# A two-layer diffusion-transformer kernel: attention and retention heads in pairs, and more of layer 0's expert activations computed before the dense stage

## The chip, the cores and the metric

One core of a Trainium2 chip. The metric is the device time of one execution in microseconds (us). The engines are named as in the profile: PE (TensorE, matrix products), PEld (its weight loads), DVE (VectorE), ACT (ScalarE), POOL (GpSimd), SP (the engine that issues most DMAs).

## The reference, cut to what matters

Two layers work on 256 tokens of `x` and, in layer 0 only, on 256 tokens of context, each of width 1024. Each layer is a mixer (layer 0: latent attention beside retention; layer 1: a gated delta rule), then a PEER block. Of the parts that change:

```
softmax_attend:  p = softmax(q k^T * scale);  o = p @ v          # 8 heads of 64 value columns
retention:       scores = (q k^T) * decay;    o = scores @ v     # 8 heads of 64
peer(h):  s1, s2 = q1 @ k1^T, q2 @ k2^T       # 8 heads x 2 halves, 128 keys each
          v1, i1 = top_k(s1, 16); v2, i2 = top_k(s2, 16)
          sc, j  = top_k(v1[:, None] + v2[None, :], 16)          # 16 experts of 16384 per head
          gate   = softmax(sc)
          act    = gelu(u_tab[e_idx] . h)
          out    = sum(gate * act * v_tab[e_idx])
```

## The kernel before, in words

**First mixer.** `attend(h)` is a generator for one attention head: query and key projections, scores `s`, softmax on DVE and ACT, transposes `pt` on PE copied to `pT` by ACT, and at last the product with the values (`oa`), 64 columns wide, which fills one half of the 128 output partitions; `put` splits the result into a high and a low part for the output projection. `retain(hp)` does two retention heads: scores `rs` (contraction over 64 partitions), decay on DVE (`sd`), product with the values (`or`, 64 columns), then a group norm. Each head's matmuls are issued by themselves. `weave` and `pipe` interleave the generators: three attention heads at a time, and one step of retention (two pairs at a time) behind each step.

**PEER, `route`.** It does not gather experts for most tokens. For 128 chunks of 128 experts it computes activations of all tokens (`act`: 24 matmuls a chunk, 384 columns each in layer 0, 256 in layer 1), multiplies them by a dense weight table `W` of gates in DRAM, and multiplies by the value table (`f`). `choose` projects the queries (`pq`, PE), takes scores (`sc`) and finds the 16 largest of each (`top`, DVE: MAX8, FIND_INDEX8, MATCH_REPLACE8). `decode`, `place` and `slots` turn the picks into columns, and `spread` builds `W`: DVE and ACT make one-hot tiles `O` and `A`, PE multiplies them (`wp`), ACT copies the product to `wst`, a DMA on SP's queue writes it. In layer 0 this covers three token blocks; the fourth (`Rows`) gathers its 128 expert rows of u and of v by indirect DMAs on POOL's queue (`rowu`, `rowv`, 512 KB each) and reduces them on DVE, one slot per step of a generator `steps`.

**PEER, `Dense`.** A table of u or v is read by SP's queue, ACT makes its high part (`ush`, `vsh`), DVE its low part (`usl`, `vsl`), and each product is three matmuls (high x high, high x low, low x high). `early` computes the activations of the first chunks ahead of time (12 in layer 0, 24 in layer 1), all kept in SBUF: `LEAD` says how many of its steps (a quarter chunk, 6 matmuls, each) are issued between the choice and `decode`, the rest goes one step per step of `spread`. `run` then goes over all chunks: activations of a pair of chunks that are not done yet, `weighted` (load of v, product of gelu and W, splits), and the `f` matmuls of the pair before. `fill` puts other work at given chunks: layer 0's affine step on POOL at chunk 2, 56 units of modulation weights (`adat`, 512 KB each, one or two DVE reductions) every second chunk from 12 on, and the 136 gather steps evenly over chunks 8 to 119.

**What sets the order.** The code's order is a priority: the Tile framework plans the instructions, takes for each engine the first in the code that is ready by its own model and whose buffers are free, and fixes each engine's queue in that order. Work can so come earlier than the code has it: the last gather steps run at 1413 us, 325 us before the dense stage ends, though the code puts them at chunk 119 of 128. On the chip each queue is strictly in order.

Lines: the matmul call 256; splits 270 (ACT) and 273 (DVE or POOL); `attend` 641, `retain` 705; `route` 799, with `top16` 816 to 822, `project` 829, `choose` 868, `decode` 884, `place` 923, `spread` 954; `Dense.act` 1076, gelu 1088, `weighted` 1098 to 1108; the gathers 1042, their reductions 1049 and 1059; `fill` 1649 to 1668; affine 422 and 423.

Of the kernel before, what the change touches and what calls it, by code (L numbers as in the profile page):

```python
# [21 lines left out]
P = 128  # L22
D = 1024
# [12 lines left out]
EARLY = 12, 24  # L36
LEAD = 15, 45
BUFS = 2, 3
LO = 'v', 'v'
# [8 lines left out]
SB = 2  # L48
# [196 lines left out]
class Model:  # L245
# [219 lines left out]
    def mixer0(self, open_x, open_h):  # L465
# [173 lines left out]


        def attend(h):
# [42 lines left out]
            for s in range(2):  # L684
                pT = p.tile([P, 2 * (s + 1), T], F32, tag=f"pT{s}", name=f"pT{s}{h}")
# [19 lines left out]
        def retain(hp):  # L705
            p = pr_
            oo = None
            for z in range(2):
# [5 lines left out]
                rows = slice(z * 64, z * 64 + 64)  # L714
                sds = []
                for s, b0, dec in ((0, 0, ds), (1, 0, dc), (1, 2, ds)):
                    o = ps.tile([P, 2, T], F32, tag="ps", name=f"rs{h}{s}{b0}")
                    for sb in range(2):
                        k0 = (b0 + sb) * P
                        self.mm(o[:, sb, :], rk[rows, hp, k0:k0 + P], rq[rows, hp, s * T:(s + 1) * T])  # L720
                    sd = p.tile([P, 2, T], F32, tag="sd", name=f"sd{h}{s}{b0}", bufs=6)
                    nc.vector.tensor_mul(sd, o, dec)
                    sds.append((s, b0, sd))
                    yield
                if oo is None:
                    oo = ps.tile([P, T2], F32, tag="ps", name=f"or{hp}")
                for s, b0, sd in sds:
                    for sb in range(2):
                        first, last = sb == 0 and b0 == 0, sb == 1 and (s == 0 or b0 == 2)
                        self.mm(oo[rows, s * T:(s + 1) * T], rv[:, b0 + sb, h * 64:(h + 1) * 64], sd[:, sb, :], first, last)  # L730
                yield
# [24 lines left out]
        rest = pipe([retain(hp) for hp in range(4)], 2)  # L756
# [42 lines left out]
    def route(self, l, hs, parts, ps, first, pd, early, rows=None):  # L799
# [3 lines left out]
        wd = self.dram.tile([len(spread_tbs) * P // WG, P, NE, WG], F32, name=f"W{l}")  # L803
        es = ExitStack()
# [8 lines left out]
        kT = pq.tile([P, 16, P], F32, name=f"kT{l}", bufs=1)  # L813
# [13 lines left out]


        def project(part, j):
# [8 lines left out]
            q = pq.tile([P, N], F32, tag="q", name="pqs" + u)  # L838
# [5 lines left out]
            S = scores[part, j] = pq.tile([P, N], F32, tag="S", name="S" + u, bufs=SB)  # L844
# [23 lines left out]
        def choose(part):  # L868
            pr = pipe([project(part, j) for j in range(16)], 2)
# [14 lines left out]
        def decode(part):  # L884
# [13 lines left out]
            nc.vector.tensor_mul(g, g, gs.unsqueeze(2).broadcast_to([P, n * NH, TOPK]))  # L898

# [16 lines left out]
            nc.vector.tensor_tensor(rb, jf[:, 0], rb, ALU.subtract)  # L916
            If = p.tile([P, n, NH, 2, TOPK], F16, tag="If", bufs=min(2, len(parts)), name="If" + u)
# [5 lines left out]
        def place(tb, n):  # L923
# [8 lines left out]
            for w in (8, 4, 2):  # L932
                nc.vector.tensor_add(eq[:, :, :w], eq[:, :, :w], eq[:, :, w:2 * w])
            ii = p.tile([P, P], F32, tag="ii", name=f"ii{t}{n}")
# [51 lines left out]
        work = choose(0)  # L986
        for part, tbs in enumerate(parts):
            weave(work)
            if part + 1 < len(parts):
                work, lead = choose(part + 1), 2 * AHEAD  # L990
            else:
                eq_.close()
                work, lead = early(), LEAD[l]
            for _ in range(lead):
                next(work)
# [3 lines left out]
            for i, tb in enumerate(tbs):  # L999
# [4 lines left out]
                weave(spread(tb, SHARE[l]), until=work)  # L1004
# [58 lines left out]
    class Dense:  # L1063
        G = 2

        def __init__(self, m, l, hs, nb, pool, ring):
            self.m, self.l, self.hs, self.nb, self.p, self.ring = m, l, hs, nb, pool, ring
            self.g = {}


        def early(self, es, ps):
            self.pg = self.m.pool(es, f"gelu{self.l}", 1)
            return chain.from_iterable(self.act(c, ps, "ps") for c in range(self.ring))


        def act(self, c, ps, tag, early=True):
            m, nc, l = self.m, self.m.nc, self.l
            N = self.nb * P
            ur = self.p.tile([P, KD, P], F32, tag="ur", name=f"ur{l}{c}", bufs=2)
            nc.sync.dma_start(ur, m.a["p_u"][l, c])  # L1080
            us = m.split(self.p, ur, [P, KD, P], "us", bufs=BUFS[l], eng=nc.gpsimd if early and LO[l][c % len(LO[l])] == "p" else None)
            o = ps.tile([P, 512], F32, tag=tag, name=f"act{l}{c}")
            for k in range(KD):
                m.mm3(o[:, :N], (us[0][:, k, :], us[1][:, k, :]), (self.hs[0][:, k, :N], self.hs[1][:, k, :N]), k == 0, k == KD - 1)
# [642 lines left out]
```

## Time and profile before

| | us |
|---|---|
| median of 3 runs | 3143.77 (3142.84 to 3145.04) |
| the profiled execution | 3142.63 |
| its span, first to last instruction | 3140.7 |
| PE busy in the span | 2816.7 (90%) |
| DVE busy | 2305.4 (73%) |
| ACT busy | 1281.7 (41%) |
| POOL busy | 708.5 (23%) |
| mean granted TensorE clock | 0.940 of full speed |

A busy time is the time in which at least one instruction of that engine is under way. Matmuls overlap: a 512-column matmul is recorded as 0.39 us, but the next one starts 0.23 us later. So the number of matmuls in a stretch says more about PE's pace than its busy share. Stages by time: first mixer's heads about 190 to 331 us, output projection and norms to 390, layer 0's choice and spread to 706, its dense stage to 1740, the second mixer to 2246, layer 1's choice and spread to 2467, its dense stage to the end.

### The profile page before, as it was taken

How to read it: one execution, taken by the hardware profiler on the slowest of the kernel's cores; microseconds unless marked ns; L12 is line 12 of the kernel's file. 1: busy time of each engine (PE TensorE's matmuls, PEld its weight loads, DVE VectorE, ACT ScalarE, POOL GpSimd, SP SyncE). 2: the span in 40 equal slices, each digit the busy share in tenths (PEclk: the TensorE clock that was granted, in tenths of full speed). 3: DMA queues.
4: the chain of work that ended last, by engine and by line, in shares of the span. 5: the costliest groups of instructions: out<-in, count | busy, mean ns of one | idle time of the engine just before them, and what ended most of it. 6: DMA issues, size and time to landing. Idle time of an engine off the chain costs nothing.

```text
span 3140.7 us, 44585 instructions
## 1 busy us (share of the span) xinstructions
PE 2816.7 (90%) x16843; PEld 2443.3 (78%) x16843; DVE 2305.4 (73%) x4520; ACT 1281.7 (41%) x2145; POOL 708.5 (23%) x453
## 2 busy tenths in 40 slices
PE   8989895857999999999999887669887899999997
PEld 4756685746999998888999666668787689999997
DVE  2955689977999999994444587976799655555555
ACT  3234432753333333333333334322348454444443
POOL 2410130024545555540000234423310100000000
PEclk9999997978999999999999888779899899999999
DMA  6530321568999999994443122312336866667663
GB/s 229 187 108 21 114 75 61 198 245 307 378 382 380 384 397 400 400 362 156 156 156 118 57 63 78 95 48 81 115 128 237 264 216 210 213 210 213 210 213 108
DMA packets 257192, 626.02 MB, mean 199 GB/s; under 512 B 34800, under 2 KB 124016, under 8 KB 252496
## 3 DMA queue, kind: packets, MB, share of 16 engines
q1 hardware_dynamic: 217632, 478.58, 45.3%
q0 software_dynamic: 38768, 142.49, 11.7%
q8 instruction: 132, 2.16, 0.3%
q10 hardware_dynamic: 576, 2.10, 0.2%
q14 instruction: 84, 0.69, 0.1%
HBM read 574.86 MB, written 48.23 MB: 198 GB/s over the span
## 4 chain that ended last, share of the span: by engine, by line
PE 55%; DVE 27%; DMA 9%; issue 5%; ACT 3%; POOL 1%; SPq 0%; POOLq 0%; ACTq 0%; DVEq 0%
PE f L256 20%; PE act L256 20%; DMA ur<-p_u 3%; DMA vr<-p_v 3%; DVE adaj L343 2%; DVE usl L273 2%; DVE cv L1264 2%; PE dz L256 1%; DVE O L966 1%; DVE rowy L1059 1%; PE y L256 1%; DVE vsl L273 1%; DVE rowu L1049 1%; DVE gelu L1108 1%; PE s L256 1%
## 5 line engine op out<-in xcount | busy, mean ns | idle before, releaser
L256 PE MATMUL f<-vsh,gsh 128*128 128x512 f32 x1260 | 491.1, 395 | 36.0 <-ACT vsh L270 36.0
L256 PE MATMUL f<-vsl,gsh 128*128 128x512 f32 x1260 | 497.7, 395 | 12.7 <-DVE vsl L273 12.5
L256 PE MATMUL f<-vsh,gsl 128*128 128x512 f32 x1260 | 494.9, 393 | 0.0
L273 DVE TENSOR_TENSOR vsl<-vr,vsh 128x1024 fp32r<-128x1024 f32 x252 | 301.4, 1228 | 246.8 <-ACT vsh L270 246.3
L273 DVE TENSOR_TENSOR usl<-ur,ush 128x1024 fp32r<-128x1024 f32 x256 | 313.5, 1226 | 173.9 <-ACT ush L270 173.9
L270 ACT ACTIVATE vsh<-vr 128x1024 fp32r<-128x1024 f32 x252 | 256.6, 1053 | 339.1 <-PE f L256 233.9
L270 ACT ACTIVATE ush<-ur 128x1024 fp32r<-128x1024 f32 x256 | 270.4, 1056 | 280.3 <-PE act L256 210.4
L256 PE MATMUL act<-hp0h,usl 128*128 128x384 f32 x1024 | 346.0, 338 | 14.5 <-DVE usl L273 14.5
L256 PE MATMUL act<-hp0h,ush 128*128 128x384 f32 x1024 | 347.0, 339 | 0.6 <-ACT ush L270 0.6
L256 PE MATMUL act<-hp0l,ush 128*128 128x384 f32 x1024 | 345.4, 337 | 0.0
L256 PEld LDWEIGHTS f<-vsh,gsh 128*128 128x128 f32 x1260 | 239.0, 190 | 88.8 <-ACT vsh L270 42.1
L256 PE MATMUL act<-hp1h,usl 128*128 128x256 f32 x1024 | 293.6, 287 | 7.7 <-DVE usl L273 7.7
L256 PE MATMUL act<-hp1h,ush 128*128 128x256 f32 x1024 | 293.6, 287 | 5.5 <-ACT ush L270 5.5
L256 PE MATMUL act<-hp1l,ush 128*128 128x256 f32 x1024 | 292.2, 285 | 0.0
L256 PEld LDWEIGHTS f<-vsl,gsh 128*128 128x128 f32 x1260 | 239.3, 190 | 65.4 <-DVE vsl L273 19.2
L256 PEld LDWEIGHTS f<-vsh,gsl 128*128 128x128 f32 x1260 | 239.1, 190 | 49.6
L270 ACT ACTIVATE gsh<-gelu 128x384 fp32r<-128x384 f32 (+1 forms) x256 | 120.3, 471 | 376.4 <-DVE gelu L1108 342.3
L1042 POOL DMA_INDIRECT rowu<-p_ur,rowe x128 | 181.6, 1419 | 189.7 <-DVE rowa L1049 135.3
L1042 POOL DMA_INDIRECT rowv<-p_v,rowe x128 | 180.2, 1408 | 146.0 <-DVE rowy L1059 121.4
L256 PEld LDWEIGHTS act<-hp0h,usl 128*128 128x128 f32 x1024 | 193.8, 189 | 15.7 <-DVE usl L273 15.3
L256 PEld LDWEIGHTS act<-hp1h,usl 128*128 128x128 f32 x1024 | 199.1, 195 | 8.9 <-DVE usl L273 8.7
L256 PEld LDWEIGHTS act<-hp1h,ush 128*128 128x128 f32 x1024 | 198.9, 194 | 8.4 <-ACT ush L270 6.3
(770 smaller groups left out, 5970.8 us busy)
## 6 DMA issues: line engine op xcount, KB each, us to landing
ur<-p_u SPq DMA_DIRECT2D x256, 512.0 KB, 4.4
vr<-p_v SPq DMA_DIRECT2D x256, 512.0 KB, 4.4
adat<-ada_t SPq DMA_DIRECT2D x80, 512.0 KB, 7.1
W<-wst SPq DMA_DIRECT2D x20, 2048.0 KB, 7.1
w<-W SPq DMA_DIRECT2D x32, 768.0 KB, 9.5
wq<-p_wq SPq DMA_DIRECT2D x32, 512.0 KB, 3.4
dw<-dn_in SPq DMA_DIRECT2D x32, 512.0 KB, 3.4
w<-W SPq DMA_DIRECT2D x32, 512.0 KB, 5.6
```

Of the source, the lines that this page charges most:

```text
L256: self.nc.tensor.matmul(out, l, r, start=start, stop=stop)
L270: nc.scalar.activation(hi, x, AF.Copy)
L273: (eng or nc.vector).tensor_sub(lo, x, hi.bitcast(F32))
L343: nc.vector.tensor_tensor_reduce(j, w, self.crow[:, s, :], op0=ALU.mult, op1=ALU.add, scale=1.0, scalar=self.c["ada_c"][:, l, m, k:k + 1], ...
L966: nc.vector.tensor_tensor(pairs(O[:, n]), bc(n), iob.unsqueeze(1).broadcast_to([P, OH, 64, 2]), ALU.is_equal)
L1042: nc.gpsimd.indirect_dma_start(t, None, tabs[z], bass.IndirectOffsetOnAxis(ap=self.e[:, s:s + 1], axis=0))
L1049: nc.vector.tensor_tensor_reduce(u, u, self.h, op0=ALU.mult, op1=ALU.add, scale=1.0, scalar=0.0, accum_out=self.act[:, s:s + 1])
L1059: nc.vector.scalar_tensor_tensor(self.y, rows.pop((1, v)), self.g[:, v:v + 1], self.y, ALU.mult, ALU.add)
L1108: nc.vector.tensor_mul(gv, gv, w4[:, :, c % WC, :])
L1264: (nc.gpsimd if CONV[j] == "p" else nc.vector).scalar_tensor_tensor(co, xp[:, :ns, q:q + T], cw[:, j, q:q + 1], co, ALU.mult, ALU.add)
```

## The change

Three things, in words, then the diff's core.

1. *Heads two by two.* `attend` of an even head keeps its transposed probabilities; the odd head issues the value products of both, alternating between the two halves of the output columns. `retain` issues the score products of its two heads alternately (two PSUM tiles, contraction in partitions 0 to 63 and 64 to 127) and so for the value products. One `put` of 128 partitions in place of two of 64. Retention pairs are started at every third step.
2. *36 chunks ahead in layer 0* (12 before; layer 1 stays at 24). The steps of all but `KEEP` = 4 of them (128 steps in layer 0, 80 in layer 1) are issued beside the choice (one or two behind each step of `top` once the projections have all been issued: 51 in layer 0, 3 in layer 1), beside `decode` and `place` (4 at each of ten places in layer 0, 8 at each of six in layer 1) and beside `spread` until they are used up; the four kept chunks come last. While the choice is issued, the tables' low parts go to POOL, after that to DVE. Gelu results of chunks 4 to 35 go to DRAM by a DMA on ACT's queue, and come back in `run` by one on SP's queue, 192 KB each, through a ring of 6. The next chunk's table is asked for while the present one is multiplied.
3. *Pace.* The work at chunks is placed by a cost of 18 for a chunk whose activations are done and 36 for another: 24 modulation units over chunks 3 to 35, the other 32 over the rest; gather steps from chunk 32 on; the affine step at chunk 59; `c_row` at chunk 0. Both v tables of a pair are asked for before either is used.

```diff
-EARLY = 12, 24
-LEAD = 15, 45
+EARLY = 36, 24
+KEEP = 4
...
-            r0 = (h % 2) * 64
-            rows = slice(r0, r0 + 64)
+            if h % 2 == 0:
+                first.append(pTs)
+                return
+            both = (first.pop(0), pTs)
             o = ps.tile([P, T2], F32, tag="ps", name=f"oa{h}")
             for s in range(2):
                 nk = 2 * (s + 1)
                 for kb in range(nk):
-                    self.mm(o[rows, s * T:(s + 1) * T], VM[:, kb, h * 64:(h + 1) * 64], pTs[s][:, kb, :], kb == 0, kb == nk - 1)
-            put(h // 2, rows, o[rows])
+                    for z in range(2):
+                        self.mm(o[z * 64:z * 64 + 64, s * T:(s + 1) * T], VM[:, kb, (h - 1 + z) * 64:(h + z) * 64], both[z][s][:, kb, :], kb == 0, kb == nk - 1)
+            put(h // 2, slice(0, P), o)
...
+            for s, b0, own in ((0, 0, 0), (1, 0, 1), (1, 2, 0)):
+                os = [ps.tile([P, 2, T], F32, tag="ps", name=f"rs{hp}{z}{s}{b0}") for z in range(2)]
+                for sb in range(2):
+                    k0 = (b0 + sb) * P
+                    for z in range(2):
+                        self.mm(os[z][:, sb, :], rk[rows[z], hp, k0:k0 + P], rq[rows[z], hp, s * T:(s + 1) * T])
...
-        rest = pipe([retain(hp) for hp in range(4)], 2)
+        rest = pipe([retain(hp) for hp in range(4)], 2, 3)
...
+        pd, work = dense.p, dense.early(e2, ps)
+        beside = islice(work, (EARLY[l] - KEEP) * KD // 2)
...
+                if ends[0]:
+                    n += 1
+                    step(1 + n % 2)
...
-            for _ in range(lead):
-                next(work)
+        for part in range(len(parts)):
+            weave(choose(part))
+        eq_.close()
+        dense.by = None
...
-                weave(spread(tb, SHARE[l]), until=work)
+                weave(spread(tb, SHARE[l]), until=beside)
         weave(work)
...
+                if c < KEEP:
+                    self.gelu(c, o)
+                else:
+                    g = self.pg.tile([P, self.nb * P], F32, tag="gelus", name=f"gelus{l}{c}", bufs=3)
+                    nc.scalar.activation(g, o[:, :self.nb * P], AF.Gelu)
+                    nc.scalar.dma_start(self.away[c], g)
...
+            def fetch(c):
+                late = c >= NE - 2
+                vr = (self.p if late else pool).tile([P, D], F32, tag="ur" if late else "vr", name=f"vr{l}{c}", bufs=2)
+                nc.sync.dma_start(vr, m.a["p_v"][l, c])
+                if KEEP <= c < done:
+                    self.gelu(c, None)
+                return vr
...
+        cost = np.cumsum([18 if c < EARLY[0] else 36 for c in range(NE - 6)])
...
-            fill.setdefault(12 + 2 * i, []).append(lambda u=u: m.ada_unit(pa, *u))
+            n = 3 * KD
+            share = ahead_share * (0.1 + 0.9 * i / n) if i < n else ahead_share + (0.97 - ahead_share) * (i - n) / (len(units) - n)
+            fill.setdefault(at(share), []).append(lambda u=u: m.ada_unit(pa, *u))
...
-        fill[2] = [affine]
-        fill[5] = [lambda: m.silu_rows(pa)]
+        fill.setdefault(at(0.4), []).append(affine)
+        fill[0] = [lambda: m.silu_rows(pa)]
...
-            fill.setdefault(8 + i * 112 // (P + LAG), []).append(lambda: next(steps))
+            fill.setdefault(at(0.9 * ahead_share + (1 - 0.9 * ahead_share) * i / (P + LAG)), []).append(lambda: next(steps))
```

## Rows read from the trace of the kernel before

**Rows 1.** Stretches: us; busy us (count) of PE, PEld, DVE, ACT, POOL; clock; DMA share; GB/s

```profile
196.00:308.00 112.00, 112.00 (x486) 70.19 (x486) 62.69 (x123) 43.99 (x99) 0.00 (x0) 1.00 0.13 37
...
390.00:494.00 104.00, 103.22 (x506) 87.36 (x507) 89.91 (x630) 33.54 (x52) 35.76 (x17) 0.98 0.22 72
494.00:521.00 27.00, 12.07 (x49) 11.11 (x49) 26.90 (x181) 4.00 (x5) 0.00 (x0) 0.68 0.13 40
521.00:546.00 25.00, 10.99 (x59) 9.89 (x58) 24.69 (x49) 8.43 (x10) 0.00 (x0) 0.77 0.26 85
546.00:678.00 132.00, 101.05 (x1003) 89.15 (x1004) 131.74 (x146) 99.98 (x236) 0.13 (x1) 0.88 0.51 200
678.00:706.00 28.00, 7.73 (x45) 7.41 (x43) 11.83 (x6) 4.48 (x7) 18.66 (x10) 0.68 0.85 298
706.00:782.00 76.00, 59.77 (x227) 46.53 (x228) 57.75 (x82) 25.31 (x34) 33.30 (x25) 0.85 0.85 302
782.00:1740.00 958.00, 947.86 (x4799) 860.66 (x4798) 754.40 (x1037) 342.33 (x487) 332.07 (x234) 1.00 0.82 302
```

**Rows 2.** Groups of PE's instructions, 196 to 331 us: busy us, mean ns, idle before

```profile
L256 PE MATMUL rs<-rq,rk 64*128 64x256 f32 x96 | 27.6, 407 | 0.0
L256 PE MATMUL or<-sd,rv 128*64 128x256 f32 x96 | 22.4, 383 | 0.0
L256 PE MATMUL oa<-pT,VM 128*64 128x256 f32 x96 | 21.3, 382 | 0.0
```

**Rows 3.** Timeline of PE in the first mixer: start us, us, what

```profile
233.78 0.38 PE L256 MATMUL oa<-pT,VM 128*64 128x256 f32 x1
233.83 0.38 PE L256 MATMUL or<-sd,rv 128*64 128x256 f32 x1
233.99 0.38 PE L256 MATMUL oa<-pT,VM 128*64 128x256 f32 x1
```

**Rows 4.** Timeline of PE in the second mixer, 32-row tiles

```profile
2019.57 0.57 PE L256 MATMUL x<-r,Y 32*32 32x32 f32 x25
```

**Rows 5.** Chain of waits: pieces (start us, us, what), and shares by line for 678 to 800 us

```profile
615.01 1.26 PE wp L256 x22
...
by line: DMA vr<-p_v 33.4%; PE f L256 17.6%; PE act L256 9.4%; DMA W<-wst 8.6%; DVE gelu L1108 7.7%; DMA w<-W 7.4%; DVE vsl L273 3.9%; issue 3.6%; DVE gsl L273 3.5%; ACT vsh L270 3.5%; DVE rowu L1049 1.1%; ACT wst L981 0.4%; ACTq L270 0.1%;
...
678.07 10.48 DMA W<-wst
...
688.62 9.00 DMA w<-W
...
780.36 8.34 PE act L256 x48
788.71 8.20 PE f L256 x36
```

**Rows 6.** Groups of DVE's instructions, 782 to 1738 us

```profile
L1059 DVE SCALAR_TENSOR_TENSOR rowy<-rowv,rowg,rowy 128x1024 f32<-128x1024 f32 x124 | 158.6, 1279 | 3.4 <-DMA rowv<-p_v,rowe 3.4
...
L273 DVE TENSOR_TENSOR usl<-ur,ush 128x1024 fp32r<-128x1024 f32 x112 | 136.5, 1219 | 74.0 <-ACT ush L270 74.0
...
L343 DVE CUSTOM_DVE_ANT_0 adaj<-adat,c_row,small 128x1024 f16<-128x1024 f32 x74 | 94.5, 1278 | 1.1 <-DMA adat<-ada_t 1.1
...
L1108 DVE TENSOR_TENSOR gelu<-gelu,w 128x384 f32<-128x384 f32 x114 | 62.8, 551 | 0.9 <-ACT gelu L1088 0.8
```

**Rows 7.** Groups of POOL's instructions, 380 to 490 us (the choice)

```profile
L273 POOL TENSOR_TENSOR usl<-wq,ush 128x1024 fp32r<-128x1024 f32 x14 | 33.6, 2398 | 55.4 <-ACT ush L270 55.4
```

**Rows 8.** Groups of instructions, 540 to 700 us (spread and what follows)

```profile
L270 ACT ACTIVATE ush<-ur 128x1024 fp32r<-128x1024 f32 x10 | 10.6, 1056 | 12.4 <-DMA ur<-p_u 8.7 <-PE act L256 3.6
...
L1108 DVE TENSOR_TENSOR gelu<-gelu,w 128x384 f32<-128x384 f32 x2 | 4.4, 2255 | 3.1 <-DMA w<-W 3.1
```

**Rows 9.** A DMA issued by ACT: ns of the issue, min/median/max

```profile
L322 ACTq DMA_DIRECT2D xT<-xT x4: 335/430/454, 0.8 to 6.6; - x4
```

**Rows 10.** Layer 1's first dense stretch, columns as in rows 1

```profile
2467.00:2537.00 70.00, 67.89 (x291) 54.12 (x291) 42.27 (x62) 32.66 (x45) 0.00 (x0) 0.95 0.69 218
```

More of the change, by code (lines that the diff above doesn't have):

```diff
@@ L2 @@
 from contextlib import ExitStack
-from itertools import chain, count, cycle
+from itertools import chain, count, cycle, islice
 import numpy as np
@@ L47 @@
 SHARE = 5, 5
-SB = 2
 AHEAD = 1
@@ L638, in mixer0 @@
         p = self.pool(ea, "m0at", 3)
+        first = []
         def attend(h):
@@ L795, in query, with route @@
         return self.split(pool, w, [P, KD, P], "us", bufs=BUFS[l], eng=eng)
-    def route(self, l, hs, parts, ps, first, pd, early, rows=None):
+    def route(self, l, hs, parts, ps, first, dense, e2, rows=None):
         nc, a, c = self.nc, self.a, self.c
@@ L826, in route, with step @@
         rects = ((0, 1, 16, 0), (1, 3, 8, 16), (4, 4, 4, 40), (8, 8, 1, 56))
+        def step(n):
+            for _ in range(n):
+                next(beside, None)
         def project(part, j):
@@ L1091, in run, with ahead @@
-        def run(self, wd, done, pool, psa, psv, fill, sums=None, ready=None):
-            m, nc, l, nb, G = self.m, self.m.nc, self.l, self.nb, self.G
+            m, N = self.m, self.nb * P
+            self.pg = m.pool(es, f"gelu{self.l}", 1)
+            self.by = m.nc.gpsimd
+            self.away = {c: m.dram.tile([P, N], F32, name=f"gelud{self.l}{c}") for c in range(KEEP, self.done)}
+            return self.ahead([*range(KEEP, self.done), *range(KEEP)], ps)
+        def ahead(self, order, ps):
+            m, nc, l = self.m, self.m.nc, self.l
+            us = self.table(order[0])
+            for n, c in enumerate(order):
+                now, us = us, None
+                o = ps.tile([P, 512], F32, tag="ps", name=f"act{l}{c}")
+                for k in range(KD):
+                    self.product(o, now, k)
+                    if k == 1 and n + 1 < len(order):
+                        us = self.table(order[n + 1])
+                    if k % 2:
+                        yield
+                if c < KEEP:
[4 more added lines that the diff above has]
+                    nc.scalar.dma_start(self.away[c], g)
@@ L1093, in run, with act @@
+        def act(self, c, ps, tag):
+            us = self.table(c)
+            o = ps.tile([P, 512], F32, tag=tag, name=f"act{self.l}{c}")
+            for k in range(KD):
+                self.product(o, us, k)
+            self.gelu(c, o)
+        def run(self, wd, pool, psa, psv, fill, sums=None, ready=None):
+            m, nc, l, nb, G, done = self.m, self.m.nc, self.l, self.nb, self.G, self.done
             N = nb * P
@@ L1639, in build @@
         dense = m.Dense(m, 0, h, 3, *pools0, EARLY[0])
-        wd = m.route(0, h, ((0, 1, 2, 3),), ps, first, dense.p, lambda: dense.early(e2, ps), rows)
+        wd = m.route(0, h, ((0, 1, 2, 3),), ps, first, dense, e2, rows)
         ep.close()
@@ L1690, in build @@
             dense = m.Dense(m, 1, h, 2, *pools1, EARLY[1])
-            wd = m.route(1, h, ((0, 1),), ps, first, dense.p, lambda: dense.early(e2, ps))
+            wd = m.route(1, h, ((0, 1),), ps, first, dense, e2)
             ep.close()
@@ L1703, in affine @@
                     m.affine(nc.gpsimd, t, rows)
-            last = dense.run(wd, EARLY[1], *pools, {2: [affine]})
+            last = dense.run(wd, *pools, {2: [affine]})
             for tb in range(2):
```

109 lines of the change are left out of this document (52 added, 57 removed).

## The prediction

> **What bounds the kernel now.** I read the busy times by stretch first, to see which engine is full where. In the first mixer's heads PE is busy all 112 us, DVE 63, ACT 44. In the choice PE (103 of 104 us) and DVE are both full. From 494 to 678 us DVE is full in each of the three stretches and PE is not, at a granted clock of 0.68 to 0.88. From 678 to 706 everything waits, and from 706 to 782, the 12 chunks whose activations are ready, PE is busy 60 of 76 us. From 782 to 1740 PE is full at full clock [rows 1]. The chain of waits then says what a matmul costs back to back: 48 of `act` in 8.34 us and 36 of `f` in 8.20 us, each two chunks, so 4.17 and 4.10 us a chunk, 8.27 together; 958 us for 116 chunks is 8.26 [rows 1, 5]. That stretch is at PE's own pace, though DVE is busy 754 of 958 us and DMA at 302 GB/s.
>
> The sum is made against the profiled execution, 3142.63 us (span 3140.7 and 1.9 around it); the median is 3143.77, 1.1 more. About 0.2% (6.3 us) can be told from no change.
>
> **Part 1, heads in halves.** `rs`, `or` and `oa` are 96 matmul records each, and `oa` shows 21.3 us of them, 0.222 us a record [rows 2]. Three times 96 by 0.222 is 64 us of PE's 112. If two halves run side by side, up to 32 us go. For column halves a row exists: where `oa` and `or` happen to alternate, one starts 0.05 us behind the other and the pair takes 0.21 us, what one alone takes [rows 3]. For `rs`, whose halves are the contraction's, the nearest row is 32-row tiles: 25 small matmuls in 0.57 us, 0.023 us each, which a serial array would hardly do [rows 4]. So the gain lies between 0 and 32 us. I take 20: the value products in full (21), two thirds of `rs` (7), less 8 us, a quarter of the 32, for pairs that coincide already and for DVE (63 us) and ACT (44 us) taking turns in each head's chain once PE needs only 80. `put` of 128 partitions saves four copies and subtractions off the path; nothing counted. The Trainium skill's page TensorEngine Tiling (Array Packing), Key Properties, says that different tiles load and multiply in parallel; by it the sum would have all of `rs`, 4 us more. No row here shows 64-row tiles side by side.
>
> **Part 2, choice and spread.** 24 more chunks are 24 x 4.17 = 100 us of PE, moved from a stage where PE is full to one where it isn't. *PE:* until 494 it is full with projections, and the new steps are issued behind them. From 494 to 706 (212 us) it is busy 132 us, at a low clock [rows 1]. 768 `wp` at 0.057 us (22 in 1.26) are 44 us at full clock [rows 5], 12 chunks 50, the rest some 5: 99. With 100 more that is 199 at full clock, or 232 if the busy time of now stays: PE just has room, or is 20 us short. *DVE:* low parts of 36 tables; about 14 go to POOL (51 steps of a quarter chunk, and one table ahead), 22 stay against 12 now: 10 x 1.14 (start to start; 1.22 recorded [rows 6]) = 11 us in a stage that DVE fills, so the last spread product moves from 678 to about 690. *POOL:* 14 x 2.4 = 34 us beside the 36 it does in the choice [rows 1, 7]: room. It slows DVE there at most by its own 34 us, at least not at all. The row of contention is a product of two tiles that takes 2.26 us in place of 0.55 while POOL does the affine step [rows 6, 8]; the choice's MAX8 and FIND_INDEX8 have POOL's 36 us beside them now and DVE stays full, so I take 1. *ACT:* 24 high parts at 1.06 [rows 8] and gelus at 0.5, with 32 DMA issues at 0.43 [rows 9]: 50 us, with 95 free of 212 [rows 1]. *SP:* 24 more reads of u, where the DMA share is 0.13 to 0.51 [rows 1].
>
> *Then the join.* Now the last write of `W` takes 10.5 us and the read 9.0, then products slowed by POOL's affine step (DVE gelu 7.7% of 122 us, 9.4) [rows 5]. The affine step moves to chunk 59: 6 us less here, some 5 back there. The four kept chunks (16.7 us) fill the wait. First `f`: 706 + 11 + 1 - 6 + 6 for PE being tight = 718, +12. Bounds: -6, and +55 (20 for PE, 34 for POOL, 1).
>
> **Part 3, the dense stage.** 24 chunks lose 100 us of PE; 92 chunks at 8.26 remain, 760 us. The open price is a chunk whose activations are ready. PE needs 4.10 us; layer 1's such stretch gives 70 us for 24 chunks of 12 `f`, 2.92 against 2.73, a factor of 1.07 [rows 10], so 4.4 here; the 12 of now took 76 us, 6.33 each [rows 1], with a third of 122 us on the chain waiting for v's landing [rows 5]. A chunk now reads v (0.52 MB), its gelu (0.20), `W` (0.20, a quarter of 768 KB) and 24/36 of a modulation unit (0.35): 1.27 MB, at 4.4 us 288 GB/s, against 302 at a DMA share of 0.85 in the stretch of 6.33 [rows 1]. DVE needs low part and two short products, 2.3 us, and 48 reductions of 1.28 [rows 6] over 36 chunks, 1.7: 4.0, no slack. I take 5.0, nearer to layer 1's since the gathers have their place behind: 180 us. The gathers (two DVE operations of 1.2 to 1.3 us a slot [rows 6]) then have 760 us; now they end at 1413, within some 700 us and in the same company, with PE full, and DVE's whole load is 812 - 27 = 785 us of 945. They cost nothing under that cover; if DVE fell behind, they would be late before the last norm, up to 25 us. Affine step: 5. Stage: 180 + 760 + 5 = 945 against 1034: -89. Bounds -116 (4.4 us) and -21 (6.33, and 25 late).
>
> **Part 4, layer 1.** The same 24 chunks; 20 results go out and back (0.43 us of ACT each, 9 us beside PE and DVE), POOL takes one or two low parts, and the last four chunks fill the join as some do now. 0, bounds -6 and +8.
>
> **Sum:** -20 + 12 - 89 + 0 = -97: 3142.6 - 97 = **3046 us**. All good ends together give 2983, all bad ones 3185.
>
> **Rivals.**
> *A, the ready chunks stay held by DMA.* The pace is a priority only; before, the last gather ran 30 chunks early. If gathers, reloads and modulation crowd v again, 36 chunks cost 6.33: +48, 3094. For: the third of the chain on v's landing. Against: the first of these chunks also had 1 MB of affine rows, and the gather rings to fill. 20%.
> *B, the mixer's heads become bound by evacuation.* Pairs finish sooner, but every product must still be read by DVE or ACT, and each head's chain passes five times between engines: 5 us gained in place of 20, 3061. Against: DVE's 63 of 112 us. The Trainium skill speaks for it (TensorEngine Tiling (Array Packing), PSUM Bottleneck: tiling quickens the matmuls, not the copying out). 14%.
> *C, slower: activations stand in front of the spread.* PE's queue is in order and 75 of the 128 steps are issued before the first spread. When a table's low part waits in DVE's queue behind a spread group (132 us / 24 = 5.5 us [rows 1]), PE stands, the two buffers of `O` and `A` fill, and DVE stands as well. If each of the 22 tables on DVE costs a whole group: +121, 3167. It decides from 97/22 = 4.4 us a table. For: DVE is full there, and PE is not. Against: one table is asked for ahead, and the plan orders DVE's queue by the same priorities. 8%.
> *D, the halves do not run side by side* in this code: 3066. 7%, since rows 3 show it for columns.
>
> **How the numbers follow.** Forecast 47%, A 20, B 14, D 7, C 8; 4% for A with the bad ends of part 2, about no change. All but C and that are faster: 0.88; same 0.04; slower 0.08. The range from 3000 to 3105 holds the forecast but for its best corner, A, B and D; left out are C, the no-change case and part of the ends of A, together near 2 in 10.
>
> **What would show it.** Right: `rs`, `or`, `oa` near half their busy time, and the heads' stretch some 20 us shorter; PE at full clock from 494 on, with first `f` near 718 of the old clock (698 with the mixer's gain); 36 chunks in some 180 us; then 8.26 us a chunk to the end; gathers ending within 100 us of it. Wrong: a chain full of v's landing after the join (A), PE waiting on low parts among the spread (C), DVE or ACT releasing most of the heads' matmuls (B), or a tail in which the last norm waits for `rowy`.

## The result, and the profile after

The changed kernel takes 3102.4 us, the median of 4 runs (3091.6 to 3114.1), beside 3144.4 for the kernel before: ratio 0.9867, 95% interval 0.9823 to 0.9911; five more runs gave 0.9862 (0.9840 to 0.9884). So it is 42 us faster, where 97 were forecast. The profiled execution is the fastest of the four, 3091.57 us (span 3089.8), 50.9 less than the span before. Its marks, the first and last start or end of a tile in the timeline:

| | before | after | difference | forecast |
|---|---|---|---|---|
| first `pq` (end of the mixer) | 390.2 | 368.4 | -21.8 | -20 |
| first `pq` to first `f` | 316.0 | 352.3 | +36.3 | +12 |
| first `f` to last `f` (dense stage) | 1044.9 | 986.6 | -58.3 | -89 |
| last `f` to layer 1's first `pq` | 494.5 | 497.4 | +2.9 | 0 |
| layer 1's first `pq` to the end | 895.1 | 885.1 | -10.0 | 0 |

Stretches of the changed kernel (us; busy us and count of PE, PEld, DVE, ACT, POOL; clock; DMA share; GB/s), to be read against [rows 1]:

```profile
196.00:286.00 90.00, 84.74 (x466) 55.20 (x467) 62.69 (x130) 44.84 (x99) 0.00 (x0) 0.91 0.16 50
...
368.00:497.00 129.00, 126.16 (x632) 109.27 (x632) 114.08 (x807) 41.79 (x62) 48.06 (x23) 0.98 0.27 90
497.00:557.00 60.00, 54.80 (x299) 53.78 (x300) 51.09 (x60) 22.64 (x31) 24.52 (x9) 0.94 0.49 159
557.00:694.00 137.00, 121.73 (x1157) 111.43 (x1156) 136.15 (x144) 109.12 (x250) 0.00 (x0) 0.97 0.66 251
694.00:721.00 27.00, 18.38 (x106) 18.06 (x104) 7.64 (x9) 12.07 (x15) 8.94 (x9) 0.88 0.96 358
721.00:900.00 179.00, 171.19 (x739) 137.85 (x739) 166.36 (x265) 61.12 (x86) 23.47 (x16) 0.98 0.95 332
900.00:1020.00 120.00, 117.43 (x596) 106.82 (x595) 114.64 (x149) 42.03 (x62) 73.69 (x52) 1.00 1.01 387
1020.00:1080.00 60.00, 40.80 (x178) 35.71 (x179) 47.85 (x52) 11.72 (x18) 44.34 (x28) 0.84 0.76 284
1080.00:1480.00 400.00, 380.90 (x1880) 339.88 (x1880) 369.16 (x504) 133.40 (x200) 236.86 (x164) 0.99 1.02 385
1480.00:1700.00 220.00, 219.29 (x1122) 199.30 (x1121) 100.23 (x132) 79.84 (x110) 0.00 (x0) 1.00 0.43 135
```

What to see: the choice still ends some 130 us after the first `pq` (at 521 us before, 497 now), but decode and slots, which follow it, now take 60 us where they took 25 [rows 1]; PE, busy 11 of those 25 us, is busy 55 of the 60. From 1020 to 1080 PE runs 178 matmuls in place of some 300. From 1080 to 1480 it is busy 0.95, with DVE at 0.92 and the DMA share over 1. Only from 1480, with the last row reduced, is it at its own pace again: 1122 matmuls in 220 us are, at 42 a chunk, 8.24 us a chunk, beside a DVE less than half busy.

The mixer's groups, which answer to [rows 2]:

```profile
L254 PE MATMUL rs<-rq,rk 64*128 64x256 f32 x96 | 16.4, 447 | 0.0
L254 PE MATMUL oa<-pT,VM 128*64 128x256 f32 x96 | 13.5, 438 | 0.0
L254 PE MATMUL or<-sd,rv 128*64 128x256 f32 x96 | 11.2, 384 | 0.0
```

71.3 us of busy time became 41.1. The timeline of PE shows the pairs (start us, us, what):

```profile
240.36 2.81 PE L254 MATMUL oa<-pT,VM 128*64 128x256 f32 x24
247.12 2.81 PE L254 MATMUL or<-sd,rv 128*64 128x256 f32 x24
```

That is 0.117 us a record where one cost 0.222 [rows 2]: the two column halves run side by side. The two halves of the contraction do so as well for the most part (`rs` from 27.6 to 16.4). The Trainium skill, TensorEngine Tiling (Array Packing), Key Properties, says that different tiles can load and multiply in parallel, and the trace agrees.

The dense stage, cut where the 37th chunk's first `f` starts (648 of 2304 records lie before it), `f` alone (PE, PEld, DVE; clock; DMA share; GB/s):

```profile
720.60:900.40 179.80, 156.17 (x648) 122.37 (x649) 0.00 (x0) 0.98 0.96 332
900.40:1707.40 807.00, 398.30 (x1656) 314.29 (x1656) 3.38 (x5) 0.98 0.83 306
```

The first stretch looks like the 180 us of the forecast, but it also holds 93 records of `act` for the four chunks behind, 16.2 us of PE. Without them the 36 ready chunks take 163.6 us, 4.5 each where 5.0 was forecast. The other 92 take 807.0, where the same 92, with the same `act`, took 764.0 before: 43 us more, and the forecast had 5 more there, for the affine step. The table's shortfall of 31 us in the stage is smaller than that, since the ready chunks came cheaper. Two questions follow: what costs 43 us in the 92 chunks, and what costs 24 more than forecast in the route.

### The profile page after: what moved, and what is told of

It is laid out like the page before. It is cut to its first block, busy times and chain, and to the rows that moved or that the text cites. A ratio compares the mean times of both kernels' runs of the same rounds, so it can differ in the third digit from the quotient of the medians.

```text
span 3089.8 us, 44817 instructions
## 1 busy us (share of the span) xinstructions
PE 2792.0 (90%) x16843; PEld 2424.3 (78%) x16843; DVE 2307.7 (75%) x4500; ACT 1272.9 (41%) x2141; POOL 747.8 (24%) x469
## 4 chain that ended last, share of the span: by engine, by line
PE 38%; DVE 16%; DMA 11%; issue 6%; POOL 4%; ACT 3%; POOLq 0%; SPq 0%; ACTq 0%; DVEq 0%
PE f L254 16%; PE act L254 15%; DMA vr<-p_v 3%; DMA rowv<-p_v,rowe 3%; DMA ur<-p_u 2%; DVE cv L1322 2%; PE dz L254 2%; POOL rowv L1061 1%; POOL rowu L1061 1%; DVE vsl L271 1%; DVE usl L271 1%; DVE rowy L1078 1%; DVE adaj L341 1%; DVE rowu L1068 1%; DMA adat<-ada_t 1%
## 5 line engine op out<-in xcount | busy, mean ns | idle before, releaser
L271 DVE TENSOR_TENSOR usl<-ur,ush 128x1024 fp32r<-128x1024 f32 x240 | 295.0, 1229 | 165.3 <-ACT ush L268 161.5
L1061 POOL DMA_INDIRECT rowu<-p_ur,rowe x128 | 175.2, 1369 | 279.0 <-DVE rowa L1068 182.7
L1061 POOL DMA_INDIRECT rowv<-p_v,rowe x128 | 186.9, 1460 | 95.5 <-DVE rowy L1078 72.0
```

What stands on the lines that cost most here:

```text
L271: (eng or nc.vector).tensor_sub(lo, x, hi.bitcast(F32))
L1061: nc.gpsimd.indirect_dma_start(t, None, tabs[z], bass.IndirectOffsetOnAxis(ap=self.e[:, s:s + 1], axis=0))
```

## The experiments

Each run is compared with runs of the kernel before on the same chip; the ratio is to those. "Rest" below is the time of the last 92 chunks in the trace, cut as above; it then holds the same matmuls in every run for which it is given, but for `gathers_8`, where 46 more `act` records (some 8 us) fall behind the cut.

### The mixer alone

The kernel before, with `attend`, `retain` and their weaving from the change and nothing else.

> The kernel before with the mixer's edit alone (heads two by two). My step said -20; the changed kernel's first pq stands 21.8 us earlier. If the edit is worth that by itself: first pq at 368 to 369 in place of 390.2, 3120 to 3123 us. Rival B (evacuation sets the pace): some 5 us, 3138. Rival D (halves one behind the other): 3142 to 3144. If the two parts of the change are independent, the rest of the change is then worth about -20 of the -42 measured.

3121.1 us, ratio 0.9914 (0.9901 to 0.9926): 27 us less. First `pq` at 365.7, 24.5 earlier; the route behind it takes 316.0 us and layer 1 896.7, as before. So the halves are worth 21 to 27 us. Rivals B and D fall, and of the 42 us only about 15 are left for the rest of the change.

### Without the gathered rows

The changed kernel, and the kernel before, each without the steps of `Rows`:

```diff
-        for i in range(P + LAG):
-            fill.setdefault(at(0.9 * ahead_share + (1 - 0.9 * ahead_share) * i / (P + LAG)), []).append(lambda: next(steps))
```

> The changed kernel without the 256 gathers and their DVE operations (the fourth block's expert rows are left out, its sum stays zero). My step said that the gathers cost nothing under PE's cover. If so, the rest of the dense stage stays at 800 to 810 us and the total at that of the changed kernel. Theory T5 (the gathers are the whole loss of the step): 92 chunks at 8.26 to 8.30, 760 to 764 us, the total 40 to 48 less. Rival (reloads, order of splits and the affine step lose it): 785 to 805.

> The kernel before without the gathers and their DVE operations (the fourth block's expert rows left out). My step read them as free under PE's full queue. If free: dense stage 1035 to 1045, total within 10 us of the kernel before. If they cost there what they cost after (63 us): 3083. Between, theory T7: 12 ready chunks at 5 in place of 6.9 (-22) and the other 116 at 8.27 in place of 8.30 (-4), 3115 to 3122; then the change itself makes the gathers dearer by some 35 to 40 us, since the products moved away leave fewer chunks to carry the same 128 slots.

After: 3038.1 us, ratio 0.9664 (0.9643 to 0.9685), 63 less than the changed kernel's 3101.5. Before: 3113.9, ratio 0.9902 (0.9887 to 0.9916), 31 less. The `f` of the changed kernel without rows, cut at the same chunk:

```profile
716.50:889.10 172.60, 154.28 (x648) 121.00 (x649) 0.00 (x0) 0.99 0.92 306
889.10:1652.70 763.60, 387.82 (x1656) 310.76 (x1656) 3.38 (x5) 0.99 0.50 159
```

and of the kernel before without rows:

```profile
702.40:973.20 270.80, 153.82 (x648) 122.75 (x649) 0.00 (x0) 0.97 0.78 260
973.20:1722.40 749.20, 385.64 (x1656) 309.75 (x1656) 3.36 (x5) 1.00 0.46 144
```

Without rows the rest is 763.6 us, so the rows cost 43 us there and 7 in the ready chunks. They were not free before either: 15 us of these 92 chunks, 10 of the first 36. The change made them 25 (traces) to 32 us (medians) dearer.

The rest of the loss is not the rows': without them the 92 chunks still take 14 us more than in the kernel before (763.6 against 749.2). These lie in one place. The changed kernel without rows, with the columns of the first fence:

```profile
900.00:1000.00 100.00, 89.87 (x438) 81.08 (x438) 69.17 (x101) 29.36 (x42) 20.54 (x8) 0.95 0.71 246
1000.00:1100.00 100.00, 100.00 (x510) 91.34 (x509) 43.34 (x51) 35.68 (x49) 0.00 (x0) 1.00 0.51 161
```

From 1000 us on PE keeps its own pace, as in the kernel before without rows (3049 and 3050 matmuls from 1000 to 1600). The 72 matmuls that are missing from 900 to 1000 are 14 us. There lies the affine step, which POOL does from 898 to 921 us in this run, and behind it DVE waits for modulation tables (`adat`, 31.4 us from 885 to 1000). No run without rows has the affine step elsewhere, so which of the two it is stays open. The reloads can cost little: the ready chunks take 172.6 us, 4.3 each without the `act` among them, and PE alone needs 4.10.

### The affine step

```diff
-        fill.setdefault(at(0.4), []).append(affine)
+        fill.setdefault(2, []).append(affine)
```

> The changed kernel with the affine step issued at chunk 2 in place of chunk 59. Theory 1a (POOL's queue is in order, so the affine step in the midst of the gathers holds rows back, then low parts on DVE behind them, then PE): the hole of 1020 to 1080 us, 178 products against 280 to 300, closes, the rest of the dense stage falls by 20 to 25 us, the ready chunks lose 5 to 10: 15 us less in all. Rival 1b (gathers packed too densely for DMA and DVE, the affine step only the place where it shows): the hole moves or spreads, total within 6 us of the changed kernel.

3089.4 us, ratio 0.9824 (0.9806 to 0.9842), against 0.9862 some 12 us less. Rest 781.3 (25.5 less), ready chunks 190.0 (10 more), and 282 matmuls from 1020 to 1080 us in place of 178: close to what theory 1a had. What stood in the hole, on POOL of the changed kernel (timeline; idle time before and what ended it in brackets):

```profile
1032.50 0.61 POOL L387 DMA_DIRECT2D lb<-ln_b  x1
1033.41 1.61 POOL L1061 DMA_INDIRECT rowu<-p_ur,rowe  x1 [0.30 <-issue]
1040.95 13.47 POOL L421 TENSOR_TENSOR x<-x,lb 128x1024 f32<-128x1024 f32 x4 [5.92 <-DMA lb<-ln_b]
1054.57 0.95 POOL L1061 DMA_INDIRECT rowv<-p_v,rowe  x1 [0.15 <-issue]
```

and on DVE:

```profile
1045.45 3.41 DVE L271 TENSOR_TENSOR vsl<-vr,vsh 128x1024 fp32r<-128x1024 f32 x1
...
1061.59 1.28 DVE L1078 SCALAR_TENSOR_TENSOR rowy<-rowv,rowg,rowy 128x1024 f32<-128x1024 f32 x1 [9.38 <-DMA rowv<-p_v,rowe]
```

POOL waits for `lb` and then adds for 13.47 us; the next gather, behind it in the same queue, goes out 21 us after the one before it. DVE stands 9.38 us on that row, with the next low parts behind it, and PE on those (10.58 us on `usl`). A low part on DVE takes 3.41 us beside POOL's additions, in place of 1.22. How much of the 25.5 us is this hold on the gathers is not measured: up to 14 of them can be what shows without any rows.

### Spacing the rows

With the affine step at chunk 2 the rest is still 17 us over the 764, and 32 over the 749 of the kernel before without rows, which has its affine step at chunk 2 as well. Two explanations were tried: rows too dense for DVE and DMA, and too few row buffers. The pacing runs tie the rows to their chunk (`dense.last` is the latest low part of a gelu product), by their indices, four at a time, 4 slots ahead (`hard_pace`) or 12 (`soft_pace`, with the affine step at chunk 2):

```diff
+            def free(s):
+                if s % 4 == 0 and s < P:
+                    q = slice(s, s + 4)
+                    nc.vector.scalar_tensor_tensor(self.e[:, q], dense.last[:, :4].bitcast(F32), 0.0, self.ef[:, q], ALU.mult, ALU.add)
```

or by their products, four at a time (`hold`) or one (`hold_1`), both with the affine step at chunk 2, and `hold` with two more edits (`hold_combo`). `hard_pace` leaves the affine step at chunk 59.

```diff
+                if s % 4 == 0 and s < P:
+                    nc.vector.tensor_scalar(self.act[:, s:s + 4], dense.last[:, :4].bitcast(F32), 0.0, 0.0, ALU.mult, ALU.add)
```

> The changed kernel with each four gathers' indices written on DVE behind the latest chunk's split of its gelu, so that a gather cannot start before its chunk (32 small DVE operations, some 0.1 us each). Theory 1b: gathers stretch from 604 us to some 700 or more, DMA share falls from 1.03 to 1.05 towards 0.9, and the rest of the dense stage falls from 9.06 to 8.3 to 8.6 us a chunk: 40 to 60 us less. Theory 1a: the hole at the affine step stays, 10 to 20 us less. Rival T2 (reload and byte count or DVE's load itself, whatever the spacing): no gain, or up to 10 us more.

> The affine step at chunk 2, and the gathers held to their chunks as in the first pacing run, but with each four indices freed 12 slots ahead of their product in place of 4, so that a row has some 40 us to land in place of some 15. Theory 1b' (the first pacing run lost because a row's landing of 6 to 10 us stood inside the ring's round, and dense packing is what costs): gathers end near 1620, rest of the dense stage 765 to 775 us against 781 of the run with the affine step alone, 5 to 15 us less in all. Rival (a gather costs DVE's and DMA's time wherever it lies; spreading them over more chunks gives nothing): rest of the dense stage 778 us or more, total the same or slower.

> Affine step at chunk 2, and the rows' products (not their gathers) held to their chunks: every four results are first set to zero on DVE behind the latest chunk's gelu split, so the products of these slots cannot run ahead on DVE, while a row is fetched as soon as its buffer is free. Theory 1b'' (what costs is 1.9 slots a chunk, 4.7 us of DVE beside 3.5 for the chunk itself and the modulation units, more than a chunk's 8.27; at 1.5 a chunk DVE keeps up): gathers end near 1640, PE's share in 1000 to 1480 goes from 0.95 to 0.99, rest of the dense stage 765 to 772 against 781, total 8 to 16 less than with the affine step alone. Rival (rows in DVE's order cost PE their waits at any spacing, as both pacing runs had it): rest 790 or more, total longer.

> As the run that held the rows' products, but slot by slot in place of four at once (128 one-column DVE operations, some 0.1 us each, 13 us of DVE in all). If the groups of four were what cost there (products in bursts of four, a ring of three rows of v behind them): rest of the dense stage 770 to 790, total 3075 to 3095. If rows cost PE their waits whenever they are held to a place in DVE's order: rest 825 or more, total 3130 or more.

> The same with the quarter chunks behind the first block's slots and 5 low parts on POOL. If the gains add: 8 to 16 less than the run with the three edits, 3066 to 3075; by the rival longer than 3082.

| | us | ratio (interval) | rest | last row reduced |
|---|---|---|---|---|
| affine step alone | 3089.4 | 0.9824 (0.9806 to 0.9842) | 781.3 | 1479 |
| `hard_pace` | 3169.9 | 1.0079 (1.0064 to 1.0094) | 883.1 | 1640 |
| `soft_pace` | 3137.6 | 0.9976 (0.9964 to 0.9988) | 831.3 | 1572 |
| `hold` | 3147.9 | 1.0009 (0.9996 to 1.0021) | 842.3 | 1642 |
| `hold_1` | 3124.0 | 0.9922 (0.9905 to 0.9939) | 819.6 | 1631 |
| `hold_combo` | 3141.7 | 0.9985 (0.9974 to 0.9996) | 845.0 | 1634 |

All five lost, and my theory that a wider spacing would win is refuted in each form that was tried; each of them also ties the rows to a place in DVE's order, and none spaces them without that. Bursts of four are a part of it (`hold` to `hold_1`: 23 us of the rest), not the whole. One stretch, with the columns of the first fence, of the kernel with the affine step alone:

```profile
1200.00:1479.00 279.00, 263.56 (x1312) 235.22 (x1311) 257.18 (x353) 94.40 (x140) 161.96 (x111) 0.99 1.00 377
```

and of `hold_1`:

```profile
1200.00:1479.00 279.00, 263.65 (x1289) 235.10 (x1288) 222.03 (x333) 88.84 (x134) 142.39 (x96) 0.98 0.90 319
```

Paced, DVE has 57 us to spare and DMA a tenth, and still PE does fewer matmuls: the waits moved to `rowy` on the landing of v's rows (83.0 us in 900 to 1600, the list of waits). A fourth buffer for these rows, without pacing:

```diff
-RING = 4, 3
+RING = 4, 4
```

> Affine step at chunk 2 and a fourth buffer for the gathered rows of v. Theory T4 (DVE's queue, in order, stands on a row of v that takes 9.9 us to land and is asked for three slots ahead, 18.7 us over 900 to 1480, and PE's low parts behind it): that wait falls below 8 us, the rest of the dense stage from 781 to 768 to 775, total 5 to 12 less than with the affine step alone. Rival (DMA at 391 to 400 GB/s is the cap): wait moves to u and v tables, total within 4 us.

3086.1 us, ratio 0.9813 (0.9795 to 0.9831), which can't be told from 0.9824; rest 784.0. Waits from 900 to 1480 (us, times, longest us) with three buffers:

```profile
ACT ush L268 <- DMA ur<-p_u: 45.5, 21, 4.8
...
DVE rowy L1078 <- DMA rowv<-p_v,rowe: 18.7, 18, 4.1
```

and with four:

```profile
ACT ush L268 <- DMA ur<-p_u: 60.4, 23, 7.7
...
DVE rowy L1078 <- DMA rowv<-p_v,rowe: 3.1, 1, 3.1
```

The wait went, as expected, and the time did not: u's tables wait longer in its place. That is what the rival had forecast, with DMA as the limit. What the full stretch is made of shows in the stretch with rows and without the affine step, before:

```profile
900.00:1400.00 500.00, 491.33 (x2474) 444.76 (x2473) 483.38 (x678) 176.81 (x258) 268.03 (x189) 1.00 1.02 389
```

and with the affine step at chunk 2:

```profile
1000.00:1480.00 480.00, 457.37 (x2277) 408.27 (x2275) 448.62 (x610) 161.32 (x241) 282.54 (x198) 1.00 1.01 385
```

At 42 matmuls a chunk these are 58.9 and 54.2 chunks. DVE's work a chunk is 8.21 and 8.28 us, as much as PE's own 8.24, and DMA is at its highest share in both. With DVE's idle time, 0.28 and 0.58 us a chunk, that makes 8.49 and 8.86 us a chunk. DMA is as good a candidate: at 389 and 385 GB/s a chunk moves 3.30 and 3.41 MB, and at the highest rate of any 60 us of the kernel before (404 GB/s, 1140 to 1200 us) these would take 8.2 and 8.4 us, an estimate from these numbers. No run tells the two apart. The plan packs 1.7 slots a chunk before and 2.0 after (99 and 106 `rowy`), since it has fewer modulation reductions to place there (54 and 25 `adaj`). Why DVE's idle time doubled is not settled: neither the landing of v's rows nor the spacing is shown to be the cause. Larger rings together with pacing were not tried.

### The route

`steps_later` issues no quarter chunk in `decode` and in `place` of the first block, and 6 or 7 in place of 4 in later blocks; `low_5` gives POOL 5 low parts in place of 14; `combo` is both with the affine step at chunk 2; `combo_1` is `combo` with one quarter chunk a step of the choice:

```diff
-            step(4 + 4 * l)
+            step(8 if l else 0 if tb == 0 else 6 if n else 7)
...
+            self.low -= 1
-            return m.split(self.p, ur, [P, KD, P], "us", bufs=BUFS[l], eng=self.by)
+            return m.split(self.p, ur, [P, KD, P], "us", bufs=BUFS[l], eng=None if l == 0 and self.low < 0 else self.by)
...
-                    step(1 + n % 2)
+                    step(1 if l == 0 else 1 + n % 2)
```

> The changed kernel with the 16 quarter chunks (17 us of PE at full clock) that are issued among the decode and the first block's slots issued among the later blocks' slots instead. Theory 3 (activations ahead of the transposes on PE hold back the spread): first O at 535 to 545 in place of 557, first f 10 to 18 us earlier. Rival (DVE and POOL's contention alone set the first O): first O within 4 us of 557, first f unchanged or later by the POOL work moved.

> The changed kernel with the first 5 tables' low parts on POOL in place of 14, the other 9 on DVE. Theory 3b (POOL's low parts beside decode and slots hold single DVE operations by 2.1 us each, some 9 of them, 19 us, and the same parts on DVE take 9 times 1.2, 11): the lone operations of 2.3 to 3.3 us go back to 0.3 to 1.2, first O and first f 6 to 10 us earlier. Rival (PE's queue alone sets first O): operations shorter, first O within 4 us of the changed kernel's 188.6 us after the first pq, first f the same or later.

> Affine step at chunk 2, quarter chunks issued behind the first block's slots, 5 low parts on POOL: if the three add up, 13 plus 12 plus 6 us less than the changed kernel, some 3065 to 3075; if the route's two edits share one cause (PE and DVE both full until the last write of W), 3075 to 3085.

> The run with the three edits (affine step at chunk 2, quarter chunks behind the first block's slots, 5 low parts on POOL), with one quarter chunk a step in the choice in place of one and two by turns, 34 in place of 51 in front of the first transposes. If PE's queue sets the first O: 177 us after the first pq in place becomes 160 to 166, and the last write of W some 5 to 12 us earlier, first f 0 to 10 us earlier, as the 17 left over run beside the spread and behind it on a PE that is full from 540 to 660. If DVE sets it by now: first O within 4 us of 177.

> The changed kernel once more, as the base for the runs beside it: 3090 to 3115 us, ratio to the kernel before 0.983 to 0.990.

| | us | ratio (interval) | first `pq` to first `O` | to first `f` |
|---|---|---|---|---|
| before | 3144.4 | 1 | 155.4 | 316.0 |
| changed, profiled twice | 3102.4, 3101.5 | 0.9867, 0.9862 (0.9840 to 0.9884) | 188.6, 193.7 | 352.3, 359.3 |
| `low_5` | 3101.6 | 0.9862 (0.9842 to 0.9881) | 191.4 | 357.6 |
| `steps_later` | 3089.7 | 0.9816 (0.9800 to 0.9831) | 177.5 | 345.4 |
| `combo` | 3082.1 | 0.9799 (0.9778 to 0.9820) | 177.4 | 346.0 |
| `combo_1` | 3071.6 | 0.9758 (0.9739 to 0.9777) | 158.2 | 338.9 |

DVE in the changed kernel, decode and the first `O`:

```profile
500.04 2.32 DVE L930 TENSOR_SCALAR ra<-jf 128x512 f16<-128x512 f16 x1
503.12 2.77 DVE L932 SCALAR_TENSOR_TENSOR ra<-jf,ra 128x512 f16<-128x512 f16 x1
...
550.50 0.41 DVE L959 TENSOR_TENSOR ii<-eq 128x128 f32<-128x128 f16 x1 [1.08 <-PE tr L968]
556.97 1.21 DVE L990 TENSOR_TENSOR O<-iT,c_iota 128x2048 f16<-128x2048 f16 x1
```

and in `combo`, where POOL is idle by then:

```profile
496.12 0.29 DVE L930 TENSOR_SCALAR ra<-jf 128x512 f16<-128x512 f16 x1
497.17 0.69 DVE L932 SCALAR_TENSOR_TENSOR ra<-jf,ra 128x512 f16<-128x512 f16 x1
...
534.57 0.41 DVE L959 TENSOR_TENSOR ii<-eq 128x128 f32<-128x128 f16 x1 [1.09 <-PE tr L968]
539.50 1.22 DVE L990 TENSOR_TENSOR O<-iT,c_iota 128x2048 f16<-128x2048 f16 x1
```

Beside POOL's 9 low parts single operations take some 2.1 us more, nearly a whole low part of POOL (2.4 us). `low_5` gives that back, and first `O` does not move: theory 3b is right on the operations and wrong on the time. The three edits together give 0.9799, which the expectation took for a shared cause of the route's two edits; the gains measured one by one would give 0.978, at the edge of its interval, so the ratio alone does not decide, but first `O` is the same with and without the 5 low parts (177.4 and 177.5). DVE then waits for a transpose, and the transpose stands in PE's queue. On PE, changed kernel:

```profile
550.19 0.27 PE L968 MATMUL tr<-small,ii 128*128 128x128 f32 x1
```

and in `combo_1`, with 34 quarter chunks run in front of it in place of 63 (12 are moved as in `steps_later`, 17 by the single step in the choice):

```profile
520.64 0.38 PE L968 MATMUL tr<-small,ii 128*128 128x128 f32 x2
```

The first `O` moved with the count of quarter chunks in front of it, as theory 3 says (`steps_later` at 540, inside its 535 to 545; first `f` 7 to 14 us earlier for 10 to 18). First `f` followed by a part alone, since PE is then full through the spread: 58 of 60 us from 540 to 600 in `combo_1`. `combo_1` beats both kernels: its interval lies below the changed kernel's.

### How many ready chunks, and where the rows begin

`early_24` and `gathers_8` (rows from chunk 8 on, as before) have the affine step at chunk 2; `combo_48` is `combo` with 48 ready chunks (`EARLY = 48, 24`).

```diff
-EARLY = 36, 24
+EARLY = 24, 24
...
-at(0.9 * ahead_share + (1 - 0.9 * ahead_share) * i / (P + LAG))
+8 + i * 112 // (P + LAG)
```

> Affine step at chunk 2 and 24 ready chunks in place of 36. By my forecast's terms 12 chunks less of 4.17 us each move back into the full stage (+50) and the route gets back what 12 chunks cost it (PE's queue, low parts: -10 to -15): some 35 us longer than with 36. Theory T6 (the route is now full on PE and DVE both, so most of the last 12 chunks' work is only moved): first f 15 to 25 us earlier after the first pq, dense stage 35 to 40 longer, total 10 to 20 longer. If ready chunks were worth nothing beyond 24: the same total.

> The run with the three edits, with 48 ready chunks in place of 36. By my forecast's terms (4.17 us of PE a chunk out of the full stage, the route with room) 40 us less. Theory T6 (PE is full from 510 to 660, so 12 more chunks lengthen the route by 45 to 50, and the 128 slots of rows crowd 80 chunks in place of 92): total the same to 20 us longer. From 24 to 36 it was 46 us less, of which the route paid 17.

> Affine step at chunk 2 and the gathers at their old places, from chunk 8 on. If the cost is per gather wherever it lies: first 36 chunks some 10 to 20 us longer (a quarter of the gathers beside chunks of 5 us, DMA at its cap), the rest of the stage 10 to 15 shorter, total within 6 us of the run with the affine step alone. Rival A's mechanism (ready chunks held by DMA at 6.33 each): first 36 chunks 228 us or more, total 15 to 30 longer.

From 24 to 36 chunks the time goes from 3135.2 us, ratio 0.9977 (0.9966 to 0.9989), to 0.9824: 48 us less by the ratios, 4.0 a chunk, with first `f` 17.5 us later after the first `pq` and the dense stage 66.5 shorter. That is above both, my forecast's 35 and theory T6's 10 to 20. From 36 to 48 it goes from 0.9799 to 0.9817 (0.9797 to 0.9837), no gain: the route takes 60 us more (405.9 from first `pq` to first `f`) and the dense stage 52 less. `gathers_8`: 3138.7 us, ratio 0.9980 (0.9969 to 0.9992), 49 us slower than with the rows behind the ready chunks; the first 36 chunks take 235.7 us, 6.3 each without the `act` among them (4.8 with the affine step alone), the rest 791.0. Rows beside ready chunks are the dearest of all, and holding them behind is what makes these chunks worth having.

## Why the prediction was right or wrong

*Part 1 held.* Forecast -20, -21.8 in the trace, 27 by the run of the mixer alone. Of the 8 us taken off for DVE and ACT, 2 to 7 were there to be had.

*Part 2 failed in size.* +12 forecast, +36. "PE just has room" was the sum over 212 us; the order within them decides. 75 quarter chunks stand in the code ahead of the first spread (in the trace 69 run before the first `O`, 16 in the kernel before), so the first `O` already came 33 us late and the last 38, where I had the last one 11 late, on DVE. That is rival C's queue, in front of the transposes and not on low parts between the groups of the spread, at a quarter of its price. With 34 in front of the first transpose in place of 63 (`combo_1`) the first `O` is 3 us late, and first `f` still 23, on a PE that is full behind it: the term for PE was near its bound of 20 and not the 6 that I took. The join's -6 did not come either: from the landing of the last write of `W` to the first `f` 19.0 us pass, 17.7 before.

The other mis-sized term was POOL's contention, "I take 1": it is some 2.1 us for each of 9 operations, inside the bound of 34, but hidden behind PE's queue (`low_5`). I priced it by the choice, and there it is nothing: MAX8 takes 280 ns in the changed kernel's choice, beside POOL. The Trainium skill, SBUF — State Buffer, Who interferes with whom, says why the two differ: DVE shares its second pair of SBUF ports with POOL, and whichever instruction gets the pair first keeps it to its end. A DVE operation in a two-port mode needs the pair, and so does one with two SBUF inputs beside a POOL operation that reads SBUF; one with a single input outside those modes does not. The trace agrees: +2.1 us for decode's, none for MAX8.

*Part 3: the step that failed is "They cost nothing under that cover", said of the gathers.* The rows cost 43 us of the 92 chunks, 807.0 with them and 763.6 without. I set DVE's load for the stage (785 of 945 us) against PE's. But the rows lie in 600 of these us, and there DVE's work a chunk is 8.2 to 8.3 us, no less than PE's, with DMA at its highest rate; the end of the stage, with DVE half idle, hid it in the mean. Which of the two holds PE there stays open.

The kernel before paid too, 31 us, and I had read the opposite from its row. "958 us for 116 chunks is 8.26" is wrong: these 958 us hold 2727 `act` and 2040 `f` records, 113.5 chunks, so 8.44 us each, and the 0.17 over PE's own 8.27 are 19 us in all. So my 760 for 92 chunks was no price of PE alone. That 763.6 without rows comes near 760 and 5 is luck: the same chunks take 749.2 in the kernel before without rows, and 14 lie at the affine step and the modulation tables. The 179.8 for my 180 is luck as well, with 16.2 us of other chunks' `act` in it; the ready chunks were cheaper, 4.5 us for 5.0.

The affine step, "5 back there", was 25 in the rest: I priced its DVE contention and not the gathers queued behind it on POOL (these 25 us lie within the 43 and the 14, not beside them). Nor did the rows end within 100 us of the stage's end: the last is reduced at 1486, 221 before it, since the code's places bind the plan no more than before.

*Part 4.* Layer 1 took 10 us less where 0 was forecast: 8 less from its first `pq` to its first `O`, 10 more from there to its first `f`, 12 less behind that. Nothing was tried on that.

Rival A did not happen, since the rows were held behind the ready chunks; with the rows among them (`gathers_8`), its 6.33 us came back as 6.3.

## What to carry to other kernels

Set an engine's load against another's in the very stretch where the moved work lies, since the mean of a stage hides one that is full in a part of it. Count the matmuls in a stretch before dividing its time by chunks, since work of other chunks may lie in it. Work "beside" a full engine is only moved, so count what stands in that engine's in-order queue ahead of the first instruction that the next stage needs. Don't put a long job into a queue that feeds prefetches.

## What the runs showed of the hardware

Two things that I had not expected. A DVE operation of 0.29 us takes 2.32 beside a low part of 2.4 on POOL, and the same holds for an f16 operation on two tiles (0.69 to 2.77) and, beside POOL's additions, for fp32 splits (1.22 to 3.41), while MAX8 does not slow beside POOL's low parts (280 ns, 283 before). And a lower DMA share does not make a gathered row land sooner by much: its median from issue to landing from 1100 to 1400 us is 9.7 to 9.9 us with the share at 1.0 (affine step alone) and 7.5 to 8.0 in `hard_pace` at 0.85 to 0.92, so pacing bought some 2 us a row in that run, which was slower all the same.
